# Where attention begins and ends in a two-layer fp32 kernel: key transposes, units ahead of the first head, output steps ahead of the last products

## The chip, the cores and the metric

One core of a Trainium2 chip runs the whole program in one launch. The metric is the device time of one execution in microseconds (us). The engines are TensorE (PE in the profile, its weight loads PEld), VectorE (DVE), ScalarE (ACT), GpSimd (POOL) and SyncE (SP). Each engine takes its instructions in the order in which they stand in its own list, and waits where one of them needs something that another engine or a transfer has not yet delivered. SP and POOL issue the transfers (DMA).

## What is computed

Two layers over a sequence of 256 tokens of width 2048, with a context of 256 more tokens; the inputs and the result are fp32. The first layer is an FFT mixer, the second an attention layer; each begins with a norm that a condition vector scales and shifts, and ends with a gated residual. The change is in the second layer, which in the reference is, cut to what matters:

```python
q, k, v, z = jnp.split(h @ w_in, [4096, 4096 + 512, 4096 + 1024], axis=-1)
kc, vc = jnp.split(hc @ w_in[:, 4096:4096 + 1024], 2, axis=-1)     # context keys, values
q = _axial_rope(q.reshape(1, n, 64, 64), rows, cols)               # 64 query heads of 64
k = _axial_rope(k.reshape(1, n, 8, 64), rows, cols)                # 8 key heads
# per block of 128 queries: masked scores over own keys and context keys
s = einsum('bqhgd,bkhd->bhgqk', q, k) * 64 ** -0.5
p = softmax(concatenate([where(mask, s, -1e30), sink]))[..., :-1]  # one sink a head
o = einsum('bhgqk,bkhd->bqhgd', p, v)
y = o.reshape(1, n, 4096) * silu(z)
x = x + gate * (y @ w_out[1])
return _rmsnorm(x, final_g)
```

## The kernel before

**Precision.** Every fp32 operand of a large product is split into a high and a low part, and each product is three matmuls (`mm3`, L78 to L80: high times high, high times low, low times high). Weights come in loads of 1 MB (`raw`, L46 to L50, three buffers, issued on SP as L49). Each half of such a load is turned into its high part by a cast on ScalarE (L65, `wh<-raw`) and its low part by a subtraction on VectorE (L66, `wl<-raw,wh`); six buffers hold the parts.

**Keys and values.** The second layer first projects keys and values for four blocks of 128 tokens (two of the sequence, two of the context) into all eight PSUM banks (L911 to L923). Then the banks are emptied: values to two bf16 tiles, keys to `kr`, through the rope on VectorE for the two sequence blocks (`roped`, L876 to L885) and by a copy for the context blocks (L941). After that, 16 transposes on TensorE (L946) bring the keys into `kT`, 64 rows a head; ScalarE copies each of the four groups out of PSUM. `prep_kk` splits one key head's rows into `kkh` and `kkl`.

**Units.** All other projections of the layer are cut into units, which `units()` (L1023 to L1040) puts in one list: 64 query units (eight for each key head, 12 matmuls each), 64 z units (two for each of 32 column blocks), and 12 "o" units, each one k step of `y @ w_out` for the output columns 0 to 511 (six matmuls). `emit_unit()` emits the next of the list and asks for the weights of the one behind it. When a key head's eighth query unit is through, `finish_q` ropes the queries and puts two query transposes on a list, `defer`.

**The attention loop.** There are 64 query heads; an index i runs over them, and the prediction calls their stages S(i) and O(i). `stage_s(i)` is four score matmuls (L1134, L1135), the mask with a row minimum on VectorE (L1136), the exponentials on ScalarE (L1139, L1140), the sum and its reciprocal, and for each of the two token blocks a tile `f`, the probabilities in two fp16 parts (high on ScalarE, L1146, low on VectorE, L1147). Each `f` is turned by one DMA transpose, issued on SP (L1148), into a half of the tile `ft`: T(i)a and T(i)b in the prediction. `stage_o(i)` is twelve matmuls of `ft` with the values (L1156 to L1158), a copy of the lower half of the result (`ot`, L1163) and an addition (L1164); where the second head of a column block is through, the block is multiplied with silu(z) into `y1` (L1119). The tiles `p`, `f` and `ft` have three buffers each; a stage S takes two of `p`, two of `f` and one of `ft`.

Ten units go ahead of the loop (`first`, L1169). In the loop, pass i emits S(i), one unit, O(i - 2), and one unit. A scheduler then orders the emitted instructions of each engine by a model of their times, so the built order need not be the one in the text; buffers that are taken again and results that are read become waits.

**The tail.** `o1_step(k)` multiplies step k of `y` with its weights into the two PSUM banks `oA`, and calls `y_split` for the steps up to k + 4: a cast and a subtraction make a high and a low tile of 128 rows. Steps 0 to 15 go into the buffers of the layer's input (`h1`), which come free with the last z matmul, steps 16 to 23 into the general pool `act`, the later ones into a pool that opens only behind the loop. That pool, `fin`, takes the memory of the loop's tiles. It holds `gbc` and `fg`, two 1 MB broadcasts (gate and final norm, L1198 and L1205); with the eight 256 KB loads of `x1d` (the residual, L1203, into `act` tiles) they are issued on POOL. Behind the loop the remaining output steps run (12 to 31), then the output columns 512 and on with weights `wo1b` and `wo1c`, and the end of the norm.

Of the kernel before, what the change touches and what calls it, by code (L numbers as in the profile page):

```python
# [10 lines left out]
F32 = mybir.dt.float32  # L11
# [7 lines left out]
P = 128  # L19
# [3 lines left out]
NB = DB // P  # L23
# [8 lines left out]
def tile_dit(ctx: ExitStack, tc: tile.TileContext, a: dict, out: bass.AP):  # L32
# [10 lines left out]
    def psum():  # L43
        return pp.tile([P, 512], F32, tag="ps", name="ps")
# [9 lines left out]
    def act(dt=F32):  # L54
        return actp.tile([P, 512], dt, tag="act", name="act")
# [44 lines left out]
    ident = const.tile([P, P], F32, name="ident")  # L100
# [786 lines left out]
    with tc.tile_pool(name="h1", reuse_waits="tile", bufs=16) as h1p:  # L887
# [3 lines left out]
        with tc.tile_pool(name="kvp", reuse_waits="tile", bufs=2) as kvp:  # L891
            hc1 = []
            for k in range(KT):
                hx = h1p.tile([P, 512], F32R, tag="h1", name="h1")
                hc = kvp.tile([P, 512], F32R, tag="h1c", name="h1c", bufs=16)
                t = kvp.tile([P, 512], F32, tag="ht", name="ht")
                for s, h in ((0, hx), (1, hc)):
                    q = slice(s * N, (s + 1) * N)
                    V.scalar_tensor_tensor(t[:, q], x1[k][:, q], gs1[:, k, s : s + 1], r_bc1[:, q] if k else r_ps[s], op0=ALU.mult, op1=ALU.mult)
                    a_ = S.activation(h[:, 0:N], t[:, q], AF.Identity, bias=sh1[:, k, s : s + 1]).ins  # L900
                    if s == 0:
                        a_end = a_
                    e = V.scalar_tensor_tensor(h[:, N : 2 * N], t[:, q], sh1[:, k, s : s + 1], h[:, 0:N].bitcast(F32), op0=ALU.add, op1=ALU.subtract).ins
                if k == 0:
                    h_end = [e] + [S.copy(r_bc1[:, i * N : (i + 1) * N], r_ps[i]) for i in range(2)]
                    with tc.issue_after(bc_end), tc.issue_after(a_end):
                        x1_turn(0, 3)
                        x1_turn(1, 3)
                hx1.append(hx)
                hc1.append(hc)  # L910
            o = [[psum() for _ in range(2)] for _ in range(4)]  # L911
            for kg in range(8):
                with tc.issue_after(h_end[0]), tc.issue_after(sq_end[0]):
                    w = ws_split(raw(a["wkv"][kg])) if kg else [w0, half_split(wr, 1)]
                for j in range(2):
                    k = kg * 2 + j
                    wh, wl = w[j]
                    for tb in range(4):
                        h = (hx1, hc1)[tb // 2][k]
                        c = (tb % 2) * P  # L920
                        for kv in range(2):
                            q = slice(kv * 512, (kv + 1) * 512)
                            mm3(o[tb][kv], h[:, c : c + P], h[:, N + c : N + c + P], wh[:, q], wl[:, q], k == 0, k == KT - 1)  # L923
            kr = []
            for tb in range(4):
                src = o[tb][1].rearrange("p (h d) -> p h d", d=64)
                va, vb = (actp.tile([P, 8, P], BF16, tag="act", name="v") for _ in range(2))
                rest = act()
                rv = rest.rearrange("p (h d) -> p h d", d=64)
                S.copy(va[:, :, 0:64], src)  # L930
                V.tensor_tensor(rv, src, va[:, :, 0:64], op=ALU.subtract)
                S.copy(va[:, :, 64:128], rv)
                GP.memset(vb[:, :, 64:128], 0.0)
                GP.tensor_tensor(vb[:, :, 0:64], rv, va[:, :, 64:128], op=ALU.subtract)
                v01.append(va)
                vlo.append(vb)
                t = kvp.tile([P, 512], F32, tag="kr", name="kr", bufs=4)
                if tb < 2:
                    roped(t, o[tb][0], tb, kvp)
                else:  # L940
                    S.copy(t, o[tb][0])  # L941
                kr.append(t)
            for hp in range(4):
                o = psum()
                for tb in range(4):
                    PE.transpose(o[:, tb * P : (tb + 1) * P], kr[tb][:, hp * P : (hp + 1) * P], ident)  # L946
                t = act()
                S.copy(t, o)
                kT.append(t)


        y1 = []
# [2 lines left out]
        with tc.tile_pool(name="at", reuse_waits="tile", bufs=2) as at:  # L955
# [19 lines left out]
            def o1_step(k, os_, wh, wl):  # L975
                while len(yh) <= min(k + 4, NB - 1) and (len(yh) < 24 or fin):
                    y_split(len(yh))
                for tb in range(2):
                    mm3(os_[tb], yh[k][:, tb * P : (tb + 1) * P], yh[k][:, N + tb * P : N + (tb + 1) * P], wh, wl, k == 0, k == NB - 1)
            slot = [0]  # L980

            def prep_kk(hk):
                kkh = at.tile([P, 512], F32R, tag="kkh", name="kkh")
# [39 lines left out]
            def units():  # L1023
                order = [("q", 0)]
                for hk in range(8):
                    if hk < 7:
                        order.append(("q", hk + 1))
                    order += [("z", b) for b in range(hk * 4, hk * 4 + 4)]
                for kind, n in order:
                    if kind == "q":  # L1030
                        oq = []
                        for kg in range(4):
                            for i in range(2):
                                yield kind, n, kg * 2 + i, oq
                    else:
                        oz = []
                        for i in range(2):
                            yield kind, n, i, oz
                for k in range(12):
                    yield "o", k // 2, k % 2, None  # L1040

            ulist = list(units())
# [16 lines left out]
            def emit_unit():  # L1059
# [18 lines left out]
                if kind == "q":  # L1078
                    if i == 0:
                        o += [psum(), psum()]  # L1080
                    if (n, i) == (0, 3):
                        with tc.issue_after(last_cast[0]):
                            prep_kk(0)
                    for j in range(2):
                        k = i * 2 + j
                        q = slice(j * 512, (j + 1) * 512)
                        for tb in range(2):
                            mm3(o[tb], hx1[k][:, tb * P : (tb + 1) * P], hx1[k][:, N + tb * P : N + (tb + 1) * P], wh[:, q], wl[:, q], k == 0, k == KT - 1)
                    if i == 7:
                        finish_q(n, o)  # L1090
                else:
                    if i == 0:
                        o.append(psum())
                    for k in range(i * 8, i * 8 + 8):
                        q = slice((k % 8) * P, (k % 8 + 1) * P)
                        for part in (0, 1) if k < KT - 1 else (1, 0):
                            if part == 0:
                                PE.matmul(o[0], wh[:, q], hx1[k], start=k == 0, stop=k == KT - 1)  # L1098
                            else:
                                PE.matmul(o[0][:, 0:N], wl[:, q], hx1[k][:, 0:N], start=False, stop=False)  # L1100
                    if i == 1:
                        th = at.tile([P, N], F32, tag="th", name="th", bufs=3)
                        zs = at.tile([P, N], F32, tag="zs", name="zs", bufs=1)
                        S.copy(zs, o[0][:, N : 2 * N])
                        V.tensor_tensor(zs, o[0][:, 0:N], zs, op=ALU.add)
                        S.activation(th, zs, AF.Tanh, scale=0.5)
                        V.scalar_tensor_tensor(th, th, 1.0, zs, op0=ALU.add, op1=ALU.mult)
                        szs[n] = th
                        emit_y(n)
# [56 lines left out]
                    obs[blk, 1] = ob  # L1166
                    emit_y(blk)

            first = 10  # L1169
            for i in range(first):  # L1170
                emit_unit()
                if i >= 8 and defer:
                    defer.pop(0)[1]()

            def filler():
                j = slot[0]
                slot[0] += 1
                emit_unit()
                if defer and defer[0][0] + 2 < j:
                    defer.pop(0)[1]()  # L1180

            pts = {}
            for i in range(66):
                if i % 8 == 0:
                    while defer:
                        defer.pop(0)[1]()
                if i < 64:
                    pts[i] = stage_s(i)
                filler()
                if i >= 2:  # L1190
                    stage_o(i - 2, pts.pop(i - 2))
                filler()


        with tc.tile_pool(name="fin", reuse_waits="tile", bufs=1) as fp:
# [22 lines left out]
                if cb < 3:  # L1218
                    GP.tensor_tensor(x, x, fg[:, q], op=ALU.mult)

            for k in range(12, NB, 2):
                w = w1_next()
                for i in range(2):
                    o1_step(k + i, oA, *(t[:, i * 512 : (i + 1) * 512] for t in w))
# [185 lines left out]
```

## Time and profile before

| what | us |
|---|---|
| median of three runs (lowest, highest) | 1826.32 (1824.57, 1828.72) |
| the profiled execution, device time | 1825.82 |
| its span, first to last instruction | 1823.8 |
| TensorE busy in the span | 1783.1 |
| mean granted TensorE clock | 0.994 of full speed |

The span is the stretch from the first to the last instruction of the profiled execution; 2.0 us of its device time lie around it. The rows that the prediction quotes come from several views of that one execution. The rows "engine line <- engine tile line" of the waits give the total of the waits in us, their number and the longest. A row of the windows gives, for a stretch of time, its length, then the busy time of TensorE, its weight loads, VectorE, ScalarE and GpSimd with the number of instructions in brackets, and at the end the granted TensorE clock, the busy share of the DMA engines and GB/s. A row of the timeline gives start, duration, engine and line, the operation, output<-input, the shape and the count, and in square brackets how long the engine stood idle before it and what released it; SPq is SP's own queue. A row of the DMA issues gives the tile or tensor, the queue, the count, the size of each and the us from issue to landing.

The attention layer's projections of keys and values end at about 1115 us; the loop runs from about 1155 to 1646 us; the output columns fill the rest.

### The profile page before, as it was taken

The numbers are of one execution on the slowest core, as the hardware profiler recorded it, in microseconds if no ns is written. First come the engines' busy times: TensorE is split into PE (matmuls) and PEld (weight loads), VectorE is DVE, ScalarE is ACT, GpSimd is POOL, SyncE is SP. The second block draws the span as 40 slices with busy tenths as digits, with TensorE's granted clock in tenths as the row PEclk, the third lists the DMA queues.
The fourth block names the chain that finished last, engine by engine and source line by source line (L and its number), as shares of the span: only waits on it lengthen the run. The fifth ranks groups of instructions, "written<-read, shape, count | busy, mean of one in ns | idle before, by whom it ended". The sixth has DMA issues, their size and how long they took to land. (4 is left out here: it accounts for less than half of the span.)

```text
span 1823.8 us, 26431 instructions
## 1 busy us (share of the span) xinstructions
PE 1783.1 (98%) x9661; PEld 1501.0 (82%) x9661; DVE 1407.4 (77%) x2774; ACT 900.6 (49%) x1535; POOL 187.0 (10%) x193
## 2 busy tenths in 40 slices
PE   6999999999999999999999999999999999997997
PEld 4679999888888888888888888788888888886886
DVE  5779888887879887767874745889889988995455
ACT  5545444522222243324322534788778877875343
POOL 0001112000000000000000002203221220300001
PEclk9999999999999999999999999999999999998999
DMA  9988889665766647653566333687888798986553
GB/s 395 417 326 236 232 242 254 220 223 225 259 237 242 241 170 294 245 208 118 193 255 257 117 113 117 185 205 191 200 203 203 200 207 193 247 199 194 187 183 138
DMA packets 209473, 399.93 MB, mean 219 GB/s; under 512 B 156288, under 2 KB 156688, under 8 KB 174272
## 3 DMA queue, kind: packets, MB, share of 16 engines
q1 hardware_dynamic: 185280, 360.24, 61.7%
q0 software_dynamic: 19920, 31.06, 6.8%
q10 hardware_dynamic: 4144, 6.95, 1.1%
q8 instruction: 76, 1.25, 0.3%
q14 instruction: 53, 0.43, 0.1%
HBM read 352.06 MB, written 12.59 MB: 200 GB/s over the span
## 5 line engine op out<-in xcount | busy, mean ns | idle before, releaser
L65 ACT CAST wh<-raw 128x1024 fp32r<-128x1024 f32 x333 | 348.9, 1049 | 565.1 <-PE ps L79 447.6
L66 DVE TENSOR_TENSOR wl<-raw,wh 128x1024 fp32r<-128x1024 f32 x333 | 422.6, 1271 | 240.5 <-ACT wh L65 237.1
L79 PE MATMUL ps<-act,wh 128*128 128x512 f32 x1024 | 398.2, 389 | 0.0
L78 PE MATMUL ps<-act,wh 128*128 128x512 f32 x1024 | 393.7, 389 | 0.0
L80 PE MATMUL ps<-act,wl 128*128 128x512 f32 x1024 | 392.8, 389 | 0.0
L80 PEld LDWEIGHTS ps<-act,wl 128*128 128x128 f32 x1024 | 192.2, 188 | 39.9
L79 PEld LDWEIGHTS ps<-act,wh 128*128 128x128 f32 x1024 | 192.2, 188 | 39.8
L78 PEld LDWEIGHTS ps<-act,wh 128*128 128x128 f32 x1024 | 192.2, 188 | 39.7
L1098 PE MATMUL ps<-h,wh 128*128 128x512 f32 x512 | 185.8, 400 | 0.0
L686 DVE CUSTOM_DVE_ANT_0 raw<-raw,cb 128x512 f32<-128x512 f32 x256 | 172.7, 689 | 13.0 <-DMA raw<-in_adw 9.5
L686 DVE CUSTOM_DVE_ANT_0 junk<-raw,cb 128x512 f32<-128x512 f32 x192 | 132.1, 688 | 24.2 <-DMA raw<-in_adw 12.9
L1100 PE MATMUL ps<-h,wl 128*128 128x256 f32 x512 | 138.2, 280 | 0.0
L78 PE MATMUL ps<-wh,h 128*128 128x512 f32 x320 | 125.7, 398 | 0.0
L79 PE MATMUL ps<-wl,h 128*128 128x512 f32 x320 | 124.9, 390 | 0.0
L80 PE MATMUL ps<-wh,h 128*128 128x512 f32 x320 | 124.0, 390 | 0.0
L1098 PEld LDWEIGHTS ps<-h,wh 128*128 128x128 f32 x512 | 96.2, 188 | 20.0
L1147 DVE SCALAR_TENSOR_TENSOR f<-p,sm,f 128x512 f16<-128x512 f32 x128 | 99.1, 807 | 11.9 <-ACT f L1146 11.4
L1139 ACT ACTIVATE p<-ps,mx 128x512 f32<-128x512 f32 x128 | 87.8, 687 | 36.5 <-DVE mx L1136 35.4
L1136 DVE CUSTOM_DVE_ANT_0 ps<-ps,mask,nsink 128x512 f32<-128x512 f32 x128 | 92.9, 752 | 9.6 <-PE ps L1135 9.0
L1100 PEld LDWEIGHTS ps<-h,wl 128*128 128x128 f32 x512 | 96.7, 189 | 2.6
L1146 ACT ACTIVATE f<-p,sm 128x512 f16<-128x512 f32 x128 | 87.6, 717 | 20.5 <-DMA ft<-f 18.7
L1156 PE MATMUL ps<-ft,v 128*128 128x256 f16 x256 | 71.3, 279 | 12.0 <-DMA ft<-f 9.8
(325 smaller groups left out, 3461.2 us busy)
## 6 DMA issues: line engine op xcount, KB each, us to landing
raw<-in_wz SPq DMA_DIRECT2D x64, 1024.0 KB, 5.5
raw<-in_adw SPq DMA_DIRECT2D x64, 1024.0 KB, 4.9
raw<-in_awp SPq DMA_DIRECT2D x32, 1024.0 KB, 12.8
raw<-in_wo SPq DMA_DIRECT2D x32, 1024.0 KB, 6.1
raw<-in_wq SPq DMA_DIRECT2D x32, 1024.0 KB, 5.4
raw<-in_wu SPq DMA_DIRECT2D x32, 1016.0 KB, 6.0
raw<-in_wo1b SPq DMA_DIRECT2D x16, 1024.0 KB, 4.9
act<-in_xT POOLq DMA_DIRECT2D x32, 256.0 KB, 6.6
```

The lines of the kernel that those rows point to most:

```text
L65: last_cast[0] = S.copy(h, src).ins
L66: last_sub[0] = V.tensor_tensor(l, src, h.bitcast(F32), op=ALU.subtract).ins
L78: PE.matmul(o, wh, xh, start=start, stop=False)
L79: PE.matmul(o, wh, xl, start=False, stop=False)
L80: return PE.matmul(o, wl, xh, start=False, stop=stop).ins
L686: V.tensor_tensor_reduce(junk if s == 0 and i < 3 else wf, wf, cb[:, s, kq * 512 : kq * 512 + 512], 1.0, 0.0, ALU.mult, ALU.add, acc[:, i, ...
L1098: PE.matmul(o[0], wh[:, q], hx1[k], start=k == 0, stop=k == KT - 1)
L1100: PE.matmul(o[0][:, 0:N], wl[:, q], hx1[k][:, 0:N], start=False, stop=False)
L1136: V.tensor_tensor_reduce(o, o, mask[:, tb, :], -0.125, nsink[:, i : i + 1], ALU.add, ALU.min, mx[:, tb : tb + 1])
L1139: S.activation(pt[tb], so[tb], AF.Exp, bias=mx[:, tb : tb + 1], scale=-1.0, accum_out=sm[:, tb : tb + 1])
L1146: S.activation(f[:, 0:512], pt[tb], AF.Copy, scale=sm[:, tb : tb + 1])
L1147: V.scalar_tensor_tensor(f[:, 512:1024], pt[tb], sm[:, tb : tb + 1], f[:, 0:512], op0=ALU.mult, op1=ALU.subtract)
```

## The change

Five edits, in the attention layer alone. The roped keys (`kr`) and the scratch of the rope move from the pool of the key and value projection, with four buffers of their own, to the general pool `act`. The 16 key transposes with their four copies, so far directly behind the emptying of the PSUM banks, become a function `k_turn(hp)`, called for all four groups behind the third unit. The split of the first key head (`prep_kk(0)`) goes from the fourth to the fifth query unit. Twelve units instead of ten go ahead of the loop. And the list of units gets 20 "o" units instead of 12: eight output steps that stood behind the loop (12 to 19) now stand in the list, so the steps behind the loop begin at 20; in the last pass (i = 65) six units are emitted ahead of O(63) and none behind it.

```diff
@@ keys
-                t = kvp.tile([P, 512], F32, tag="kr", name="kr", bufs=4)
+                t = act()
                 if tb < 2:
-                    roped(t, o[tb][0], tb, kvp)
+                    roped(t, o[tb][0], tb, actp, "act")
                 else:
                     S.copy(t, o[tb][0])
                 kr.append(t)
-            for hp in range(4):
-                o = psum()
-                for tb in range(4):
-                    PE.transpose(o[:, tb * P : (tb + 1) * P], kr[tb][:, hp * P : (hp + 1) * P], ident)
-                t = act()
-                S.copy(t, o)
-                kT.append(t)
@@
+            def k_turn(hp):
+                o = psum()
+                for tb in range(4):
+                    PE.transpose(o[:, tb * P : (tb + 1) * P], kr[tb][:, hp * P : (hp + 1) * P], ident)
+                t = act()
+                S.copy(t, o)
+                kT.append(t)
@@ units
-                for k in range(12):
+                for k in range(20):
                     yield "o", k // 2, k % 2, None
@@ emit_unit
-                    if (n, i) == (0, 3):
+                    if (n, i) == (0, 4):
                         with tc.issue_after(last_cast[0]):
                             prep_kk(0)
@@ the loop
-            first = 10
+            first = 12
             for i in range(first):
                 emit_unit()
+                if i == 2:
+                    for hp in range(4):
+                        k_turn(hp)
                 if i >= 8 and defer:
                     defer.pop(0)[1]()
@@
                     pts[i] = stage_s(i)
                 filler()
+                if i == 65:
+                    for _ in range(6):
+                        filler()
                 if i >= 2:
                     stage_o(i - 2, pts.pop(i - 2))
-                filler()
+                if i < 65:
+                    filler()
@@ behind the loop
-            for k in range(12, NB, 2):
+            for k in range(20, NB, 2):
                 w = w1_next()
```

The lines of the kernel after lie some lines on: L946 becomes L978, L1134 to L1136 become L1135 to L1137, L1146 to L1148 become L1147 to L1149, L1156 to L1158 become L1157 to L1159, L1198, L1203 and L1205 become L1206, L1211 and L1213.

## The prediction

> **What bounds the kernel now.** I read the page first, then the waits of TensorE, then the windows, then the timeline and the DMA landings at each wait.
>
> ```profile
> span 1823.8 us, 26431 instructions
> PE 1783.1 (98%) x9661; PEld 1501.0 (82%) x9661; DVE 1407.4 (77%) x2774; ACT 900.6 (49%) x1535; POOL 187.0 (10%) x193
> ...
> PE ps L78 <- DVE dh L184: 12.6, 2, 11.3
> PE ps L1156 <- DMA ft<-f: 9.8, 1, 9.8
> PE ps L1156 <- ACT f L1146: 2.2, 1, 2.2
> ...
> PE ps L946 <- DVE kr L885: 1.0, 1, 1.0
> ...
> 1165.00:1170.00 5.00, 2.82 (x16) 1.80 (x15) 3.71 (x6) 3.27 (x7) 4.25 (x4) 0.81 0.96 253
> 1170.00:1175.00 5.00, 5.00 (x25) 4.24 (x24) 3.73 (x10) 3.74 (x9) 4.92 (x5) 0.85 0.65 144
> 1200.00:1300.00 100.00, 100.00 (x556) 83.27 (x554) 87.99 (x166) 79.78 (x153) 19.96 (x15) 1.00 0.81 201
> ...
> 1650.00:1655.00 5.00, 0.00 (x0) 0.00 (x0) 0.26 (x1) 0.00 (x0) 0.00 (x0) 0.50 1.05 329
> 1655.00:1660.00 5.00, 3.90 (x16) 2.94 (x17) 3.76 (x10) 3.53 (x10) 0.00 (x0) 0.54 0.90 123
> ```
>
> TensorE is busy in 1783.1 of 1823.8 us, so a change can only win from its idle time or its clock. In the body of the attention (the window from 1200) it is busy 100.00 of 100.00 us at full clock: whatever the change reorders there is worth nothing. The 12.6 us belong to the first, FFT-like layer. What is left to this change are three places: **A**, the key transposes (1.0 us); **B**, the first head's products with v (2.2 us); **C**, the last heads' products (9.8 us). The clock column adds to B and C: 0.81 and 0.85 in two windows of 5 us behind B's idle time lose (0.19 + 0.15) x 5 = 1.7 us of full-speed work. At C the column stays near a half to about 1659.6, while matmuls begin at 1656.1: 3.5 us at half speed, 1.75 us lost. So A costs 1.0, B 2.2 + 1.7 = 3.9, C 9.8 + 1.75 = 11.5.
>
> The change issues the same matmuls, splits, loads, scores, products and output steps as before, the 16 key transposes and their 4 copies too. Nothing is added or taken away, so the sum has only terms of order. I name the score group of pair i S(i), its two DMA transposes T(i)a and T(i)b, and its twelve products O(i).
>
> **A, key turning.**
>
> ```profile
> 1115.00 0.39 PE L80 MATMUL ps<-wh,h1c 128*128 128x512 f32 x1
> 1116.42 0.63 PE L946 MATMUL ps<-ident,kr 128*128 128x128 f32 x4 [1.04 <-DVE kr L885]
> 1116.81 0.49 PE L78 MATMUL ps<-wh,h 128*128 128x512 f32 x1
> ...
> 1115.00:1120.00 5.00, 3.96 (x20) 3.04 (x19) 5.00 (x6) 3.11 (x5) 3.71 (x5) 1.00 0.42 177
> ```
>
> Before, the first four transposes stand directly behind the last matmul of the kv projection and wait for the rope on VectorE, which is busy 5.00 of these 5 us. In the built order of the changed kernel the two first query units (24 matmuls of 512 columns) come in between, then 2, 8 and 6 transposes. From 1160.06 to 1165.27 (rows below) 24 matmuls start 0.2265 us apart, so the cover is 24 x 0.2265 = 5.4 us, against the 1.4 us from 1115.00 to 1116.42. The idle 1.04 goes. What is late next is VectorE: the rope still ends at its old time, and the third query unit's low weight half is subtracted behind it; it is wanted behind 24 matmuls, ten transposes of 0.1 (four from 1116.42 to 1116.81) and two matmuls more, at about 1115.2 + 5.4 + 1.5 = 1122.1, and I can place it no better than 0 to 2 us ahead of that. If that cover fails, the wait comes back there with its old price. Gain 1.0, from 0 to 1.4 (the whole gap between the two starts). The roped keys now sit in the pool of activations instead of their own; the pool has free tiles at this point, which I cost at nothing within that same bound.
>
> **B, twelve units ahead of the first head.**
>
> ```profile
> 1155.75 0.39 PE L1134 MATMUL ps<-kkh,qa 128*128 128x512 f32 x1
> 1160.06 0.39 PE L78 MATMUL ps<-wh,h 128*128 128x512 f32 x1
> ...
> 1165.27 0.39 PE L80 MATMUL ps<-wh,h 128*128 128x512 f32 x1
> 1167.84 0.27 PE L1156 MATMUL ps<-ft,v 128*128 128x256 f16 x1 [2.18 <-ACT f L1146]
> ...
> 1163.17 2.71 SPq L1148 DMA_TRANSPOSE ft<-f  x2
> 1165.98 0.53 SPq L49 DMA_DIRECT2D raw<-in_wz  x1
> ...
> ft<-f SPq DMA_TRANSPOSE x2, 3.2
> ...
> 1300.13 0.40 PE L1098 MATMUL ps<-h,wh 128*128 128x512 f32 x1
> 1300.48 0.40 PE L1098 MATMUL ps<-h,wh 128*128 128x512 f32 x1
> ...
> 1634.75 0.48 SPq L49 DMA_DIRECT2D raw<-in_wo1a  x1
> 1635.41 1.24 SPq L1148 DMA_TRANSPOSE ft<-f  x1
> ...
> ft<-f SPq DMA_TRANSPOSE x1, 6.9
> ```
>
> Before, between S0 and O0 stand S1, 7 matmuls, S2 and 24 matmuls: TensorE is at O0 9.75 us after S0 began (1155.75 to 1165.5). T0a goes out at 1163.17, T0b some 1.4 us later, and it lands 3.2 us on, at about 1167.8, 12.0 us after S0; the label of the row names ScalarE, but the landing fits to 0.1 us. In the changed kernel the order is S0, 7, S1, 24, S2, then 32 of the z units' matmuls. A pair of those takes 0.35 us (1300.13 to 1300.48), so 3 x 0.91 + 7 x 0.2265 + 24 x 0.2265 + 16 x 0.35 = 15.3 us: 5.6 us more cover than before, for a wait of 2.2. With the old landing the whole wait would go. But SP's order changes too: one raw weight load now stands ahead of T0a, and SP issues in order. It waits for a weight split on VectorE; before, the load that stands there went at 1165.98, 10.2 us after S0; T0a's data were there at 7.4. So it goes between 7.4 and 10.2. A transpose behind a load landed at 1635.41 + 6.9 = 1642.3, 7.6 us after that load's issue at 1634.75. O0's data are then there at 15.0 to 17.8, against 15.3: a wait of 0 to 2.5, I take 1.0 (the split is early rather than late: VectorE has 5.6 us more matmuls to hide under). That is less than half of 2.18 and near A's 1.04, behind which the clock stayed at 1.00, so I charge no half clock. Gain 3.9 - 1.0 = 2.9, from 0 (2.2 us of wait and its clock remain) to 3.9.
>
> [...]
>
> **C, the last heads.**
>
> ```profile
> 1642.05 0.51 SPq L49 DMA_DIRECT2D raw<-in_wo1a  x1
> 1645.86 12.10 SPq L1148 DMA_TRANSPOSE ft<-f  x4
> ...
> 1645.98 0.54 POOL L1198 DMA_DIRECT2D gbc<-gated  x1 [75.26 <-DVE f L1147]
> 1646.52 0.54 POOL L1205 DMA_DIRECT2D fg<-in_fg  x1
> ...
> 1644.84 0.28 PE L1156 MATMUL ps<-ft,v 128*128 128x256 f16 x1
> ...
> 1646.05 0.27 PE L1158 MATMUL ps<-ft,v 128*128 128x256 f16 x1
> 1656.10 0.37 PE L1156 MATMUL ps<-ft,v 128*128 128x256 f16 x1 [9.78 <-DMA ft<-f]
> ...
> 1655.19 0.72 ACT L1146 ACTIVATE f<-p,sm 128x512 f16<-128x512 f32 x1 [5.78 <-DMA ft<-f]
> 1655.82 2.53 ACT L65 CAST act<-act 128x256 fp32r<-128x256 f32 x8
> ...
> gbc<-gated POOLq DMA_DIRECT2D x1, 1024.0 KB, 5.5
> fg<-in_fg POOLq DMA_DIRECT2D x1, 1024.0 KB, 7.8
> ft<-f SPq DMA_TRANSPOSE x1, 9.3
> ...
> ft<-f SPq DMA_TRANSPOSE x1, 3.1
> ```
>
> The wait of O62 is a collision. The two broadcasts gbc and fg (1 MB each) wait on POOL; the row names f, 75 us back, but the built program has them wait for memory that the last scores, S63, free as well. They go at 1645.98 and 1646.52. T62a goes 0.1 us ahead of them and lands after 9.3 us, where a transpose alone lands in 3.1 (one at 1617). The DMA engines are full meanwhile (1.05 in the window from 1650). T62b comes right behind, and O62 starts at 1656.10, 10.1 us after gbc's issue. The order before is S63, O61, O62, some 22 output matmuls, O63.
>
> The changed kernel moves output matmuls from behind to ahead: its tail runs S61, 17, O59, S62, O60, S63, O61, 23, O62, 17, O63. So O62 and O63 get 5.2 us and 3.9 us of cover and, as T62 and T63 follow T61 directly on SP with no load between, I let their waits go. But now O61 stands right behind S63, where O62 stood before but for twelve products. From the end of S61 to O61 TensorE has 17 x 0.2265 + 2 x 1.3 + 2 x 0.91 = 8.3 us (twelve products 1.3 us: from 1644.84 to 1646.05 are eleven steps of 0.11). S0 ended at 1155.75 + 4 x 0.2265 = 1156.66 and its T0b went out 7.9 us later; with 3.1 to land, T61b is due 11 us after S61, nearly 3 us after TensorE is at O61, even alone. And it is not alone: S63 ends at about 7 to 8.3 us, gbc went 1.2 us after S63's end before (O61, directly behind S63, began at 1644.84), so the broadcasts start at 8 to 9.5 while T61a and T61b are on their way, behind the last raw load of this stage, which also stands ahead of T61a on SP. I therefore give T61 the landing that T62 had: O61 waits 9.5 us (3 if T61 is through first, 10.5 if T60's landing, which the buffers of f tie to T61, is late too), and half clock at 1.75 as now. Behind it comes work that the wait before hid: ScalarE stands in f of the next pair until a T lands (5.78 us before) and only then casts the eight y tiles (2.53 us) that the next output matmuls read. Before, O62's twelve products at half clock (2.5 us) covered that; behind O61 the copy of its result and a softmax piece go first, about 1.5 us more (0 to 3). O60 may wait for T60b, 0.6 (0 to 2). In sum 9.5 + 1.75 + 1.5 + 0.6 = 13.3 against 11.5: a **loss of 1.8**, between a gain of 8.5 and a loss of 6.
>
> [...]
>
> **Sum:** -1.0 - 2.9 + 1.8 = -2.1 us against the profiled execution's 1825.82 (its span and 2.0 us around it): 1823.7. That execution lies 0.5 us below the median of the three runs, 1826.32; I say 1824.
>
> **The rivals.** *R1, T61 is through before the broadcasts:* T62a had 0.1 us of lead on gbc; T61b, issued 7.9 us after S61 with gbc at 9.5, would have 1.6. Against it speak the raw load ahead and f's three buffers, which take most of that. Then O61 waits 3 us instead of O62's 9.8, with at most one half-clock stretch of 1.7: C goes from 11.5 to 3 + 1.7 + 1 = 5.7, and the whole comes to -3.9 - 5.8 = -9.7, 1816.
>
> *R2, slower: two waits in a row.* T59 and T60 stand on SP behind a raw load whose split is late; O60 then waits for T60b as a transpose behind a load does (6.9 against 3.1: 3.8 us more), S63 and with it gbc and fg go later by as much, and O61 waits its 9.5 nonetheless, with half clock behind both (1.7 more). C becomes 13.3 + 3.8 + 1.7 = 18.8, +7.3; with A and B +3.4 or, with B's gain cut by half, +5: about 1830. It decides from the point where O60's wait is over 2 us. The eight loads of x1d (2 MB), which now wait for tiles of the y splits and so go in the last 50 us, push the same way. Against it: 53 output matmuls (12 us) between S60 and S61.
>
> *R3, the units ahead don't do what they should:* the raw load ahead of T0a goes as late as 10.2 us, and O0 waits 2.5 us as before, half clock and all. Then -1.0 + 1.8 = +0.8: 1826.6.
>
> **How the numbers follow.** Forecast 0.47 (1820 to 1827.5 by its own bounds), R1 0.25, R2 0.20, R3 0.08. A measurement of this kernel can tell 0.2%, 3.65 us, from no change. Faster than 1822.7: all of R1 and a third of the forecast's case, 0.41. Slower than 1830: half or more of R2 and its upper tail, with a little of the forecast's, 0.22. Between: 0.37. The range takes in R1 but for its best part and R2 up to one wait more: 1815 to 1831.
>
> **What would show it.** A: no wait of the key transposes for kr, TensorE without a gap at 1115. B: a wait of O0 under 1.3 us and clock 1.00 after it. C: one long wait of the products, at O61 instead of O62, of 9 to 10 us, with gbc and fg issued within 2 us of T61b; O62 and O63 without one. Wrong, if the products' longest wait in the tail is near 3 us (R1), if two of them are over 2 (R2), or if any wait in the body is new.

## The result, and the profile after

The kernel got slower: 1829.66 us in the median of 18 runs (1825.05 to 1834.10) against 1826.42 (18 runs, 1824.43 to 1829.40) of the kernel before on the same chip. The ratio is 1.0018, with a 95% interval of 1.0011 to 1.0026: 3.2 us, clear of zero though under the 0.2% named above. The spread nearly doubled, from 5 us to 9.

The profiled execution lies at the upper end of that spread: 1833.0 us, span 1830.8, so 7.0 us over the span of before. First its waits of TensorE, in the form of the prediction's rows (total in us, times, longest):

```profile
span 1830.8 us, 26425 instructions
...
PE ps L1157 <- DMA ft<-f: 14.9, 5, 8.8
...
PE ps L216 <- DMA raw<-in_awp: 3.8, 5, 1.7
PE ps L78 <- ACT act L65: 1.6, 1, 1.6
PE ps L1157 <- ACT f L1147: 0.9, 1, 0.9
```

The wait for `kr` is gone. The products (L1157 here) wait for DMA transposes five times instead of once, 14.9 us instead of 9.8. The 3.8 at L216 belongs to the first layer, which the change doesn't touch; before, the same line waited 2.6 us for weights and 1.3 us under another label. The same stretches of both executions, before first (length, busy time of TensorE first, the granted clock third from the end):

```profile
1100.00:1200.00 100.00, 96.78 (x490) 80.41 (x490) 75.82 (x117) 64.27 (x111) 22.94 (x18) 0.98 0.57 168
...
1500.00:1600.00 100.00, 100.00 (x588) 84.88 (x587) 90.44 (x173) 79.53 (x156) 18.18 (x18) 1.00 0.89 222
1600.00:1640.00 40.00, 40.00 (x221) 33.24 (x220) 36.45 (x77) 32.90 (x70) 0.00 (x0) 1.00 0.78 195
1640.00:1680.00 40.00, 30.22 (x149) 23.93 (x149) 23.04 (x47) 19.79 (x42) 1.08 (x2) 0.87 0.71 196
```

and after:

```profile
1100.00:1200.00 100.00, 99.34 (x508) 83.36 (x507) 76.03 (x115) 64.47 (x109) 26.22 (x18) 1.00 0.58 164
...
1500.00:1600.00 100.00, 97.58 (x572) 81.75 (x571) 89.87 (x167) 75.80 (x151) 14.26 (x11) 1.00 0.91 199
1600.00:1640.00 40.00, 31.18 (x157) 25.34 (x157) 29.48 (x67) 25.72 (x60) 3.83 (x7) 0.87 0.82 179
1640.00:1680.00 40.00, 33.83 (x179) 26.35 (x178) 28.60 (x62) 26.36 (x56) 1.07 (x2) 0.96 0.92 239
```

The idle time of TensorE (length less busy) by stretch: 3.2 became 0.7 at the start of the attention layer; 0 became 2.4 in 1500 to 1600 and 8.8 in 1600 to 1640, which had none before; and 9.8 became 6.2 at the end. In sum 13.0 became 18.1. The start behaves as forecast and the end is better than forecast (a loss was forecast there). The loss stands in between, where the prediction saw nothing.

Where the 8.8 us are: the timeline of TensorE, of SP's queue and of POOL around that wait, and two rows of the DMA landings (the transpose issued at 1615.05, and the one at 1656.30):

```profile
1618.71 0.61 PE L78 MATMUL ps<-wh,ys 128*128 128x512 f32 x2
1628.15 0.39 PE L1157 MATMUL ps<-ft,v 128*128 128x256 f16 x1 [8.82 <-DMA ft<-f]
...
1610.96 0.33 SPq L49 DMA_DIRECT2D raw<-in_wo1a  x1
1612.90 6.00 SPq L1149 DMA_TRANSPOSE ft<-f  x2
...
1608.28 0.56 POOL L1211 DMA_DIRECT2D act<-x1d  x1 [41.90 <-DVE ys L66]
...
1611.57 0.55 POOL L1211 DMA_DIRECT2D act<-x1d  x1 [1.27 <-DVE ys L66]
1615.81 1.88 POOL L1211 DMA_DIRECT2D act<-x1d  x3 [3.70 <-DVE ys L66]
...
ft<-f SPq DMA_TRANSPOSE x1, 13.1
...
ft<-f SPq DMA_TRANSPOSE x1, 3.8
```

The product that waits is O57. Its second transpose goes out at 1615.05 and lands 13.1 us later, at 1628.1. Around it are seven loads of `x1d` on POOL's queue, released by VectorE's `ys` (the y splits), as the new y tiles 16 to 23 take the free `act` buffers first. The granted clock then stays at 0.50 from 1622.8 to 1633.0, so the matmuls from 1628.15 on ran for 4.9 us at half speed (O57's products start 0.21 us apart, those of O0 0.11 apart at a clock of 1.00), and 2.4 us more were lost. The end, from the same execution:

```profile
1660.27 0.37 PE L1157 MATMUL ps<-ft,v 128*128 128x256 f16 x1 [3.67 <-DMA ft<-f]
1664.60 0.50 PE L78 MATMUL ps<-wh,act 128*128 128x512 f32 x1 [1.61 <-ACT act L65]
...
1657.58 0.54 POOL L1206 DMA_DIRECT2D gbc<-gated  x1 [39.89 <-PE ps L1136]
```

O61 waits 3.67 us, not 9.5: T61b went out at 1656.30, 1.3 us ahead of gbc, and landed in 3.8.

### The profile page after: what moved, and what is told of

It is laid out like the page before. It is cut to its first block, busy times and chain, and to the rows that moved or that the text cites. A ratio compares the mean times of both kernels' runs of the same rounds, so it can differ in the third digit from the quotient of the medians.

```text
span 1830.8 us, 26425 instructions
## 1 busy us (share of the span) xinstructions
PE 1785.2 (98%) x9661; PEld 1501.6 (82%) x9661; DVE 1424.2 (78%) x2774; ACT 896.5 (49%) x1535; POOL 190.3 (10%) x193
## 4 chain that ended last, share of the span: by engine, by line
PE 89%; DMA 6%; DVE 2%; ACT 1%; issue 1%; ACTq 0%; POOL 0%; POOLq 0%; DVEq 0%; SPq 0%
PE ps L78 24%; PE ps L79 24%; PE ps L80 24%; PE ps L1099 5%; DMA ft<-f 3%; PE ps L1101 3%; DMA raw<-in_awp 2%; PE ps L1157 1%; PE ps L1158 1%; PE ps L1159 1%; PE ps L1135 1%; PE ps L1136 1%; PE ps L216 1%; DVE f L1148 1%; DMA dm<-in_dmat 0%
## 5 line engine op out<-in xcount | busy, mean ns | idle before, releaser
L66 DVE TENSOR_TENSOR wl<-raw,wh 128x1024 fp32r<-128x1024 f32 x333 | 427.2, 1285 | 236.9 <-ACT wh L65 234.4
L686 DVE CUSTOM_DVE_ANT_0 raw<-raw,cb 128x512 f32<-128x512 f32 x256 | 172.4, 688 | 10.4 <-DMA raw<-in_adw 6.9
L1148 DVE SCALAR_TENSOR_TENSOR f<-p,sm,f 128x512 f16<-128x512 f32 x128 | 104.9, 849 | 12.0 <-ACT f L1147 12.0
L1147 ACT ACTIVATE f<-p,sm 128x512 f16<-128x512 f32 x128 | 87.6, 716 | 36.1 <-DMA ft<-f 19.7
L1137 DVE CUSTOM_DVE_ANT_0 ps<-ps,mask,nsink 128x512 f32<-128x512 f32 x128 | 92.2, 748 | 2.2 <-PE ps L1136 2.2
L1157 PE MATMUL ps<-ft,v 128*128 128x256 f16 x256 | 71.4, 279 | 15.8 <-DMA ft<-f 14.9
```

The costliest lines, as they stand in the source:

```text
L66: last_sub[0] = V.tensor_tensor(l, src, h.bitcast(F32), op=ALU.subtract).ins
L686: V.tensor_tensor_reduce(junk if s == 0 and i < 3 else wf, wf, cb[:, s, kq * 512 : kq * 512 + 512], 1.0, 0.0, ALU.mult, ALU.add, acc[:, i, ...
L1137: V.tensor_tensor_reduce(o, o, mask[:, tb, :], -0.125, nsink[:, i : i + 1], ALU.add, ALU.min, mx[:, tb : tb + 1])
L1148: V.scalar_tensor_tensor(f[:, 512:1024], pt[tb], sm[:, tb : tb + 1], f[:, 0:512], op0=ALU.mult, op1=ALU.subtract)
L1157: PE.matmul(oo[:, 0:N], v01[kb][:, hk, :], fh, start=kb == 0, stop=False)
```

## The experiments

All times are medians in us; the ratio is to the kernel before on the same chip, with its 95% interval.

| kernel | time | ratio | longest waits of products (us) |
|---|---|---|---|
| after | 1829.66 | 1.0018 (1.0011 to 1.0026) | O57 8.8, O61 3.7 |
| after, x1d early | 1832.29 | 1.0033 (1.0021 to 1.0044) | O50 8.0, O61 3.6 |
| after, x1d on SP, last | 1834.86 | 1.0037 (1.0017 to 1.0057) | O61 15.7 |
| start only | 1832.12 | 1.0024 (1.0013 to 1.0035) | O50 7.2, O61 3.6 |
| output steps only | 1830.11 | 1.0013 (1.0002 to 1.0024) | O62 12.0 |
| after, all late loads on SP, last | 1824.01 | 0.9982 (0.9973 to 0.9992) | O61 3.6 |
| before, gbc and fg on SP, last | 1820.71 | 0.9962 (0.9949 to 0.9975) | O62 4.6 |
| after, gbc and fg on SP, last | 1830.34 | 1.0019 (1.0009 to 1.0028) | O57 5.4, O61 3.6 |
| start, realigned | 1825.01 | 0.9991 (0.9982 to 1.0000) | O62 10.2 |
| start, realigned, gbc and fg on SP | 1818.63 | 0.9956 (0.9942 to 0.9970) | O62 4.6 |
| start only, gbc and fg on SP | 1830.62 | 1.0018 (1.0005 to 1.0032) | O61 3.5, O50 2.3 |
| whole change, realigned, gbc and fg on SP | 1822.75 | 0.9975 (0.9965 to 0.9986) | O62 4.6, O58 2.1 |

### First set: is it where the x1d loads fall?

**x1d early.** In the changed kernel the x1d tiles are taken, and loaded, at the first output step:

```diff
                     if n == 0 and i == 0:
                         oA.extend([psum(), psum()])
+                        for tb in range(2):
+                            x2.append([act() for _ in range(4)])
+                            for c in range(4):
+                                nc.gpsimd.dma_start(x2[tb][c], x1d[tb, :, c * 512 : (c + 1) * 512])
```

> The changed kernel with one edit: the eight x1d tiles are taken from the general pool, and their loads issued, at the first output step instead of behind the loop. Theory T: in the changed kernel the y tiles 16 to 23 take the free act tiles first, so the x1d loads (2 MB on POOL's queue) fall at the end of the z units, into the flight of T57, and O57 waits 8.8 us, with 1.75 us of half clock behind it. With the loads early again the wait of O57 is under 2 us and the time is 1818 to 1822, 8 to 11 us below the changed kernel's. Rival U: O57 waits because its f is late on VectorE and the loop's end has little cover (T57b went out 12 us after S57 instead of 8), the loads only fall at the same time; then O57 still waits 5 us or more and the time stays within 3 us of 1829.7.

**x1d on SP, last.** The eight x1d loads on SP's queue, behind the last transpose:

```diff
-                    nc.gpsimd.dma_start(x2[tb][c], ...)
+                    with tc.issue_after(last_t[0]):
+                        nc.sync.dma_start(x2[tb][c], ...)
```

> The changed kernel with one edit: the x1d loads go on SP's queue, behind the last transpose, instead of POOL's; gbc and fg stay where they are. Theory T: nothing collides with T57; O57 waits under 2 us, O61 waits 3 to 4 us as in the changed kernel's profile, and the time is 1817 to 1822. Rival U: O57's wait stays at 5 us or more, time 1827 to 1831. If 2 MB more on SP make the weights of the next columns late, a new wait stands at about 1690 us.

**Start only.** The output steps as before (`range(12)` in the list, steps 12 and on behind the loop, no six units in the last pass):

> The changed kernel with the output steps as before: 12 of them in the list, none of the six extra ones in the last pass; the key turning and the twelve units ahead stay. Its built order up to O61 is that of the changed kernel, and its x1d tiles are taken ahead of the y tiles 16 to 23, as before. Theory T: no collision at O57, the start gains 4 us, O61 waits about 4 us instead of O62's 9.8: 1816 to 1820. Rival U: O57 waits 5 us or more here too, as the order and the cover are the changed kernel's: 1826 to 1830.

**Output steps only.** The kernel before with 20 steps in the list and eight more units ahead of O63 in the last pass:

> The kernel before with the output steps alone changed: 20 in the list, the last eight ahead of O63; key turning and ten units ahead as before. The built order up to O62 is that of before (O61 and O62 side by side behind S63), but the x1d tiles are taken behind the y tiles. Theory T: the loads fall into the end of the z units and one product near O57 or O58 waits 3 to 9 us more, with half clock; O62 waits its 10 us as before; no gain at the start: 1830 to 1838. Rival U: with the order and cover of before there is no new wait: 1825 to 1828.

Theory T was right about O57 and wrong about the time. With x1d early, or on SP behind all transposes, O57 doesn't wait; but the time fell in neither (1.0033 and 1.0037, with intervals that overlap that of the changed kernel). With the loads early, another product pays. Start only, the timeline of TensorE, SP and POOL, and the landings of the transposes issued at 1556.23 and at 1557.90:

```profile
1571.20 0.37 PE L1157 MATMUL ps<-ft,v 128*128 128x256 f16 x1 [7.18 <-DMA ft<-f]
...
1554.51 0.33 SPq L49 DMA_DIRECT2D raw<-in_wz  x1
1556.23 3.31 SPq L1149 DMA_TRANSPOSE ft<-f  x2
...
1557.26 3.81 POOL L1207 DMA_DIRECT2D act<-x1d  x7
...
ft<-f SPq DMA_TRANSPOSE x1, 4.6
...
ft<-f SPq DMA_TRANSPOSE x1, 13.2
```

T50a is 1.0 us ahead of the first x1d load and lands in 4.6; T50b, 0.6 us behind it, takes 13.2, and O50 waits 7.2. So the start alone, without any new output step, already makes the kernel 4.8 us slower than before. Why did the same loads at the same place cost the kernel before nothing? Its rows for T50 and T52 on SP, seven of POOL's eight loads being at 1560.76 to 1564.57 (the last at 1570.17), and the first matmul of O52:

```profile
1547.74 0.33 SPq L49 DMA_DIRECT2D raw<-in_wz  x1
1548.44 5.17 SPq L1148 DMA_TRANSPOSE ft<-f  x2
...
1564.70 8.63 SPq L1148 DMA_TRANSPOSE ft<-f  x2
...
1577.63 0.28 PE L1156 MATMUL ps<-ft,v 128*128 128x256 f16 x1
```

T50 left at 1548.4, 6.6 us after S50 (1541.81); in the start-only kernel it left at 1556.2, 13.1 us after S50 (1543.17). In the kernel before, the loads met T52, whose second half landed 9.6 us after its issue at 1567.87, at 1577.49: 0.14 us ahead of O52. It got by with nothing to spare.

That points to the reserve. Over the passes 8 to 47 I took, from the rows of each trace, the median time from S(i) to the issue of T(i)a and from the landing of T(i)b to O(i):

| kernel | S to issue | landing to O |
|---|---|---|
| before | 7.4 | 5.0 |
| after | 10.0 | 3.3 |
| start only | 10.2 | 2.8 |

In the median the transposes go out 2.6 us later. How much reserve is left varies between executions: the second profile of the changed kernel (below) gives 11.2 and 1.7. Counting SP's issues ahead of T50, there are 260 weight loads before and 261 after: the two units taken ahead of the loop bring their weights ahead too, and this one load stays ahead of each transpose up to T61. In these passes the load just ahead of T(i)a goes out 6.4 us after S(i) before and 8.8 us after, and T(i)a follows 1.0 us behind it in both.

x1d on SP shows the other side. O61, which had waited 3.67 us, now waits 15.7:

```profile
1660.91 0.37 PE L1158 MATMUL ps<-ft,v 128*128 128x256 f16 x1 [15.72 <-DMA ft<-f]
...
1643.54 16.75 SPq L1150 DMA_TRANSPOSE ft<-f  x4
...
1645.49 0.57 POOL L1207 DMA_DIRECT2D gbc<-gated  x1 [87.96 <-PE ps L1137]
...
ft<-f SPq DMA_TRANSPOSE x1, 15.9
```

T61b went out at 1644.90, 0.6 us ahead of gbc, and took 15.9 us. With 1.3 us of lead it took 3.8. The 18 us between the fastest and the slowest run of this kernel (1824.22 to 1842.67) would fit a race decided by such a margin; one profile can't show it.

The output steps alone cost 2.8 us. They don't come between S63 and O62 at all (the built order there still has O61 and O62 side by side); they send the x1d loads to 1610 to 1619, where O58 waits 1.7, and O62 waits 12.0 instead of 9.8. On the changed start the same steps cost nothing that can be seen: the changed kernel stands at 1.0018, start only at 1.0024. With the steps O57 waits; without them the loads go early, O50 waits instead, and O63 waits 1.2.

### Second set: take the bursts away

**All late loads on SP, last.** x1d as above, gbc and fg likewise with `nc.sync` behind the last transpose.

> The changed kernel with all ten late loads (x1d, gbc, fg) on SP's queue behind the last transpose. Theory V: what the change loses is transposes that meet a burst of POOL's loads (x1d near O50 or O57, gbc and fg near O61) and land after 8 to 16 us instead of 3 to 6; which product pays depends on who is in flight. With no burst while transposes fly, no product waits more than 4 us, the start's gain of 4.4 us stays, and the time is 1812 to 1818. Rival W: the built order of the changed tail (O59 to O61 close together, O57 with thin cover) is itself the loss; then O57 or O61 still waits 5 us or more and the time is 1823 or above.

**Before, gbc and fg on SP.** The kernel before with these two alone:

```diff
-            nc.gpsimd.dma_start(gbc, gated.broadcast_to([P, D]))
+            with tc.issue_after(last_t[0]):
+                nc.sync.dma_start(gbc, gated.broadcast_to([P, D]))
```

> The kernel before with gbc and fg alone moved to SP's queue, behind the last transpose; x1d stays on POOL, where no product waited for it. Theory V: O62's wait falls from 9.8 to about 3 us, most of its half clock goes too: 1816 to 1821. Rival W (the wait at the end is the late f of S62 and S63, not the broadcasts): O62 waits 6 us or more, 1823 to 1827.

**After, gbc and fg on SP.** The same edit in the changed kernel:

> The changed kernel with gbc and fg alone moved to SP's queue; x1d stays on POOL, at the end of the z units. Theory V: the product near O57 still waits 5 to 10 us, with half clock; O61 waits about 3 us: 1822 to 1830, that is 8 us or more above the run with all ten loads moved. Rival W: both runs come out alike, within 3 us.

**The changed kernel again.** One execution, 1830.94 us.

> The changed kernel once more, for a second profile. Theory V: which product waits, and how long, is a race of a burst with two transposes, so the waits differ from the first profile by some us in place or length, though the built order is the same. Rival W: the same waits at O57 (8.8) and O61 (3.7) within 1 us.

In the kernel before, moving the two broadcasts is worth 6.3 us: O62's wait falls to 4.6. In the changed kernel it is worth nothing (1830.34): O61 waits 3.57 with the broadcasts gone and 3.67 with them. So they were no part of the changed kernel's tail, and O57 waits 5.4 as theory V asked. The time is 6.3 us above the run with all ten loads moved, where theory V asked for 8 and rival W for less than 3. The second profile has O57 at 7.3 and O61 at 3.4: the same places, with O57 1.5 us off, which lies between theory V and rival W.

With all ten loads away no product waits over 4 us, as theory V said, but the time is 1824.0, 6 us above its range. What is left is the tail itself, in the waits of that kernel:

```profile
PE ps L1158 <- DMA ft<-f: 5.7, 3, 3.6
...
PE ps L78 <- ACT act L65: 1.6, 1, 1.6
...
PE ps L1158 <- ACT f L1148: 1.4, 1, 1.4
```

O59 1.6, O60 1.4, O61 3.6, then 1.6 for the y casts behind O61: 8.2 us with no broadcast near, against 4.6 in the old tail without broadcasts. So rival W holds for part of the loss: S61 to S63 and O59 to O61 stand too close together in the changed order. And that order is the start's doing: the start-only kernel has it too, up to O61.

### Third set: give the two units back later

**Start, realigned.** The start-only kernel with one unit less in two passes of the loop:

```diff
                     stage_o(i - 2, pts.pop(i - 2))
-                filler()
+                if i not in (20, 28):
+                    filler()
```

> The start of the changed kernel (key turning, twelve units ahead), 12 output steps in the list, and one unit less in the passes 20 and 28, so that from pass 28 on the loop stands to the units as before; the built order of the tail is that of before to the instruction, and gbc, fg and x1d stay on POOL. Theory X: the two units taken ahead shift every later stage against the loads by a pass and close up S61 to O61, and this, not the start, is what the change pays for; here x1d meets no product, O62 waits its 10 us as before, and only the gain at the start is left: 1821 to 1824, 3 to 5 us under the kernel before. Rival Y: the two units ahead cost what they gain elsewhere too (a product near O50 waits 5 us or more, or the body loses): 1826 or above.

**Realigned, gbc and fg on SP:**

> The same with gbc and fg on SP's queue behind the last transpose. Theory X: the gain of the start (about 4 us) and that of the moved broadcasts (6 us in an earlier run) add: 1815 to 1819, O62 waits about 4.6 us. Rival Y: they don't add, 1820 or above.

**Start only, gbc and fg on SP:**

> The start of the changed kernel, 12 output steps, gbc and fg on SP's queue, and no unit left out later. Theory X: O50 meets x1d's loads and waits 7 us as in the run without the output steps, O60 and O61 wait 1.4 and 3.6 us, as SP's queue or POOL's makes no difference to T61, which is late by itself: 1826 to 1832, 10 us or more above the realigned one. Rival Z (the broadcasts at the end are what every slower version pays): 1822 or below.

**The whole change, realigned, gbc and fg on SP** (20 output steps in the list, eight units ahead of O63 in the last pass):

> The fastest version so far (start of the change, two units left out later, gbc and fg on SP behind the last transpose) with the change's output steps on top: 20 in the list, the last eight ahead of O63. It asks what that edit does by itself, once the start no longer shifts the tail and no broadcast meets it. Theory: the steps cover only O63, which never waited, and they send x1d's loads to the end of the z units, where a product near O57 or O58 waits 2 to 6 us more: 1820 to 1825, 2 us or more above the version without. Rival: the edit is neutral or better there, 1819 or below.

Realigned, no product between 1500 and 1640 waits, 260 weight loads stand ahead of T50 again, the time from S to the issue of T is 7.2 us again in the passes 48 to 56 (7.3 before, 10.5 after), and the built tail is that of before. The time is 1825.01, 1.4 us under the kernel before: better than every version with the shift and its loads on POOL, but less than the 3 to 5 expected; the ratio's interval ends at 1.0000, so this gain is only just seen. Its profile gains 2.6 us in span and shows where some of the rest went: O20 waits 1.1 us, with one unit less between S20 and it, and O62 10.2 where it was 9.8. With the broadcasts moved the two gains add to 7.8 us. This kernel has the lowest time of the study, and its six runs lie within 1.3 us (1818.46 to 1819.76). But its ratio (0.9956) can't be told from that of the kernel before with the broadcasts moved (0.9962): what the start itself is worth, 1.4 us alone and about 1.1 here, is at the edge of what these runs show. Its waits of products:

```profile
PE ps L1158 <- ACT act L65: 4.6, 1, 4.6
...
PE ps L1158 <- DMA ft<-f: 2.0, 3, 1.1
```

Without the realignment the same edits give 1830.62, 12.0 us more. The profiled execution of that one was the fastest of its ten (1823.62; O50 waited 2.3 there), so its waits say little of the median. The whole change on the realigned start loses 4.1 us against the version without the output steps (3.5 by the two ratios); in its profile the three waits for transposes come to 3.8 instead of 2.0, 2.1 of it at O58, next to the x1d loads; that execution took 1820.06 us, 2.7 below its median, so it shows less than the usual loss. The product that the eight steps stand ahead of, O63, waited in neither.

## Why the prediction failed

The direction was wrong: a gain of 2 us was forecast, and 3.2 were lost. That the time lies inside the range is luck, as the upper part of the range stood for R2's long waits at O60 and O61, which came to 0.9 and 3.7 us.

**A was right.** TensorE goes from the kv projection into the query units without a gap; S0 begins at 1154.71 instead of 1155.75, 1.0 us sooner.

**B was right as far as it looked.** The first product in the timeline of the changed kernel, and the two windows that stood at 0.81 and 0.85 of the clock:

```profile
1170.92 0.28 PE L1157 MATMUL ps<-ft,v 128*128 128x256 f16 x1 [0.66 <-DMA ft<-f]
...
1165.00:1170.00 5.00, 5.00 (x30) 4.29 (x28) 4.78 (x8) 3.30 (x8) 5.00 (x5) 1.00 1.05 272
1170.00:1175.00 5.00, 4.34 (x29) 3.56 (x28) 5.00 (x5) 2.98 (x6) 5.00 (x4) 1.00 0.76 232
```

O0 waits 0.66 us (1.0 was taken) and the clock stays at 1.00. The gain is 2.2 - 0.7 + 1.7 = 3.2 us (2.9 was taken). The 1.7 of clock is not lost in every execution: in the kernel before with gbc and fg on SP, whose start is the same, O0 waits 2.20 us and both windows show 1.00. And the step "one raw weight load now stands ahead of T0a" was priced for O0 alone. That load stays ahead of T1 to T61.

**The step that failed is in the first part:** "In the body of the attention ... whatever the change reorders there is worth nothing." TensorE is busy all the time there, before and after, and the sentence holds up to 1500 us. But the same rows hide how much time lies between a transpose's landing and its product, and that reserve fell from 5.0 to 3.3 us, because the transposes go out later. Before, the x1d loads at 1560 cost nothing by 0.14 us. After, the one load that still went early (1565.81) met T51 and cost 1.6 us at O51, and the rest, moved to 1608 to 1618 by the y tiles, 8.8 us at O57 and 2.4 of clock. Where no x1d load is near, in the kernels with x1d last on SP, neither O51 nor O57 waits. In the profiled execution A, B and the end come to -7.8 us (1.0, 3.2 and 3.6) and this stretch to +13.6 (2.4 and 8.8 of idle time, 2.4 of clock): 5.8 of the 7.0 us. The prediction put the body at nothing, though it named "any wait in the body" as a sign of being wrong. The x1d loads were named too, as something that would "push the same way" in R2, with no price and no product that they would meet.

**C was wrong in its largest term, and with it in its sign.** "I therefore give T61 the landing that T62 had": it had 3.8 us, and O61 waited 3.67 for 9.5 expected, as R1 had it. T61b went out 9.1 us after S61's end and gbc 10.4; the prediction had gbc at 8 to 9.5, with T61 behind the raw load and so still on its way. The smaller terms were near: 1.61 for the y casts behind O61 (1.5), 0.9 at O60 (0.6), no wait at O62 and O63. But the 5.2 us of cover that the prediction gave to O62 came from the start and not from the output steps moved ahead: 22 of the 23 matmuls between O61 and O62 are there without them. The steps cover O63, with 17 matmuls instead of 1. By the runs, they cost 2.8 us alone, 4.1 on the realigned start, and nothing that can be seen on the changed start.

**R2 had the right sign,** and 1830 as its time, but by another way: two waits in a row at O60 and O61. The prediction gave it 0.20.

What stays open: what makes up the 4.1 us that the output steps cost in the median on the realigned start, as the one profile, of a faster execution, shows some 2 us of waits; and how much of the 3.2 us falls to O57 in an average run, as two profiles (8.8 and 7.3 us there, in executions of 1833.0 and 1830.9) are both above the median.

## What to carry to other kernels

An engine that is busy all the time can stand on a reserve that a change eats (here 5.0 us, then 3.3): before work is moved ahead of a loop, measure in the trace how long each operand is there before it is used, and count what else moves past it in the queues. Work put ahead of the loop shifted the later passes here (S to issue from 7.4 to 10.2 us with the start only); as many units left out later on took that loss away (1.0024 to 0.9991). Where large loads with time to spare meet small urgent transfers, try them behind these in the same queue: in the kernel before, that was worth 6.3 us, three times the gain forecast for the change. In the changed kernel the same edit was worth nothing, as no product of its tail waited for the broadcasts.

## What the hardware showed

In the kernel with x1d on SP, T61b met the two broadcasts on POOL's queue and took 15.9 us to land, and for six of them hardly any packet began. The windows around O61's long wait there, with the DMA engines' busy share and GB/s last:

```profile
1646.00:1648.00 2.00, 0.00 (x0) 0.00 (x0) 1.98 (x7) 1.92 (x7) 0.61 (x2) 1.00 3.45 263
1648.00:1654.00 6.00, 0.00 (x0) 0.00 (x0) 1.65 (x4) 1.33 (x2) 0.00 (x0) 0.58 0.34 26
1654.00:1660.00 6.00, 0.00 (x0) 0.00 (x0) 0.00 (x0) 0.00 (x0) 0.00 (x0) 0.50 0.95 327
```

These columns count a packet in the stretch in which it begins. In the six us after 1648, with a transpose and 2 MB of broadcasts waiting, hardly any packet began (26 GB/s, against 327 right after), and the share of 3.45 says why: packets begun just before ran on. Those of POOL's queue, begun from 1647.8 to 1648.5 and then from 1654 to 1660, with their number, MB and the time they took as a share of the 16 engines' time in the stretch:

```profile
q0 software_dynamic: 16, 0.13, 925.0%
...
q0 software_dynamic: 255, 1.84, 76.2%
```

The first 16, of 8 KB each, took 6.5 us apiece (9.25 x 0.7), the later ones 0.3. The changed kernel has a milder case at O57:

```profile
1616.00:1621.00 5.00, 3.33 (x15) 2.44 (x13) 5.00 (x14) 4.36 (x11) 1.45 (x3) 1.00 1.28 183
1621.00:1625.00 4.00, 0.00 (x0) 0.00 (x0) 2.41 (x4) 0.21 (x2) 0.00 (x0) 0.72 1.16 65
```

65 GB/s at a busy share of 1.16: the packets were under way, but took long. In the kernel with x1d on SP those 16 packets of POOL's queue took some 20 times as long as the later ones (6.5 us apiece against 0.3). Neither the cause nor when it sets in was tried here. Most of these traces look as if a lead of a microsecond decided it: transposes issued 1.0 and 1.3 us ahead of a burst landed in 4.6 and 3.8 us, those 0.6 and 0.1 us ahead in 15.9 and 9.3, one 0.6 us behind in 13.2. But the lead is not all of it: with gbc and fg on SP in the start-only kernel, T50b went out 1.1 us ahead of the x1d loads and took 8.3.
